# One transformer layer on one core: both input streams loaded ahead of every adaLN tile, and the tile groups put at fixed places among the products

## The chip, the core and the metric

The kernel runs on one core of one Trainium2 chip. The metric is the device time of one execution in microseconds (us), the median of several runs. The core has a matrix engine (PE, with PEld for its weight loads), a vector engine (DVE), a scalar engine (ACT), GpSimd (POOL), and a sync engine (SP) which here does nothing but issue loads. Each engine takes its own instructions strictly in the order in which the program lists them, and waits for the others by semaphores.

## The reference, cut to what matters

One layer over 256 latent tokens `x` and 256 context tokens `ctx` of width 2048, in float32:

```python
sh1, sc1, g1, sh2, sc2, g2 = adaln(c, w_ada, b_ada)        # split(silu(c) @ w_ada + b_ada, 6)
csh1, csc1, ... = adaln(c_ctx, w_ada, b_ada)
h  = rms_norm(x,   norm_mix_g) * (1 + sc1)  + sh1
hc = rms_norm(ctx, norm_mix_g) * (1 + csc1) + csh1
y, _ = neighbourhood_attention(h, hc, w_qkv, ...)          # q from h; k, v from h and hc; 16 heads
x = x + g1 * y
hf = rms_norm(x, norm_ffn_g) * (1 + sc2) + sh2
x = x + g2 * conv_ffn(hf, w_up, conv_w, conv_b, w_down)    # 5504 hidden columns
```

## The kernel before

Activations lie with features on the partitions: `xl` and `xc` hold the two streams as 16 feature tiles of 128 by 256 tokens. A product in full float32 precision is made of three fast ones: each weight tile `wr` is split on ACT into a rounded part `wh` (a CAST) and on DVE into a remainder `wl`; the activations are split in the same way into `hh` and `hl`; and PE adds up `wh*hh`, `wl*hh` and `wh*hl` (lines 369 to 371 in `nat`, 128x512 each). The tiles rotate: four buffers for `wr`, three for `wh`, two for `wl`.

The change concerns the first stage, the first 166 us or so. The 16 feature tiles are worked off in nine steps ("grains": two of one tile, then seven of two), because shift and scale of each come from `w_ada`, 1 MB per feature tile, and that is loaded on the way. For a grain:

- `ada_step` loads its four adaLN tiles `wx` (each a quarter of the input rows; four buffers) and multiplies them with silu(c) in four groups of small matmuls (line 404, called groups below). ACT copies the sums into `ev`, PE transposes them (line 414), and DVE reduces them to `shT` and `gsT` (lines 419 to 427).
- `modulate` scales the grain's part of `xl` and `xc` on DVE (line 438), and makes `hh` on ACT (443) and `hl` on DVE (444).
- `first_products` multiplies `hh` and `hl` with three weight tiles: the first 512 columns of k, kept in four PSUM banks `pj`, and the first 1024 of v, made in two rotating banks `mx` and added up on DVE into `vsum` (line 471; for the first grain ACT copies them, line 469). It has six pieces of two token tiles each: k for latent tokens, v0 latent, k context, v0 context, v1 latent, v1 context. A piece is 6 products for a grain of one tile, and 12 for a grain of two.

The groups of the next grain are written between the pieces of this one. `stats` computes 1/rms of a stream: squares on ACT (351), sums on DVE (356) and PE (226), the power on POOL (194), and a broadcast by PE (217). In the kernel before, `xl` is loaded first, then the first grain's `wx`, two weight tiles and only then `xc`; the first grain's pieces for latent tokens are multiplied while `xc` comes in and is normalized.

All loads of weights and streams go through one queue, SP's. The order on each engine is set by a scheduler at compile time, which goes by program order, by its own estimates of durations, and by the hints in the code (`issue_after`: not before that instruction of the same engine; `high_priority`).

Of the kernel before, what the change touches and what calls it, by code (L numbers as in the profile page):

```python
# [9 lines left out]
F32 = mybir.dt.float32  # L10
# [5 lines left out]
P = 128  # L16
# [36 lines left out]
def block_kernel(  # L53
# [23 lines left out]
    def ms():  # L77
        return ps.tile([P, CH], F32, tag="ms", name="ms", bufs=2)
# [65 lines left out]
        )  # L144
        return w

    last = []

    def wpair(src, k0, kn, c0, cn):

        w = wload(src, k0, kn, c0, cn)
        hi = wp.tile([P, KT, CH], F32R, tag="wh", name="wh", bufs=3)
        lo = wp.tile([P, KT, CH], F32R, tag="wl", name="wl", bufs=2)
        a = nc.scalar.copy(hi[:, :kn, :cn], w[:, :kn, :cn])  # L154
        b = nc.vector.tensor_tensor(  # L155
            out=lo[:, :kn, :cn], in0=w[:, :kn, :cn], in1=hi[:, :kn, :cn].bitcast(F32),
            op=ALU.subtract,
        )
        last[:] = [a.ins, b.ins]
        return hi, lo  # L160

# [42 lines left out]
    def rstd_rows(pool, sums, name, copy):  # L204

        v = pool.tile([P, 2], F32, tag=name + "v", name=name + "v")
        nc.vector.tensor_scalar(
            out=v, in0=sums, scalar1=1.0 / D, scalar2=EPS, op0=ALU.mult, op1=ALU.add
        )
        r = rsqrt_newton(pool, v, 2, name, 1)  # L210
        dg = pool.tile([P, 2, P], F32, tag=name + "d", name=name + "d")
        diag = nc.vector.tensor_tensor(
            out=dg, in0=ident.unsqueeze(1).to_broadcast([P, 2, P]),
            in1=r.unsqueeze(2).to_broadcast([P, 2, P]), op=ALU.mult,
        )
        bp = mx()[:, :T]
        nc.tensor.matmul(bp, ones, dg.rearrange("p b t -> p (b t)"), start=True, stop=True)
# [103 lines left out]
    def hl(kt, t):  # L321
        return hls[kt // (KD // 2)][:, kt % (KD // 2), t]
# [38 lines left out]
    def nat(psl, tt0, w, kt0, n, first, last):  # L361

        wh, wl = w
        for i, pt in enumerate(psl):
            ts = slice((tt0 + i) * P, (tt0 + i + 1) * P)
            for k in range(n):
                kt = kt0 + k
                a, z = first and k == 0, last and k == n - 1
                nc.tensor.matmul(pt, hh[:, kt, ts], wh[:, k, :], start=a, stop=False)  # L369
                nc.tensor.matmul(pt, hh[:, kt, ts], wl[:, k, :], start=False, stop=False)  # L370
                nc.tensor.matmul(pt, hl(kt, ts), wh[:, k, :], start=False, stop=z)  # L371
            side.tick(side.rate)
            ada.tick(ada.rate)

# [10 lines left out]
    kps = [pj() for _ in range(4)]  # L385
    loads = []

    def ada_step(b0, nb, work=()):

        ap_ = ms()  # L390
        n = 2 * nb * P
        for q in range(4):
            if q < len(work):
                work[q]()
            w = xp.tile([P, 4 * CH], F32, tag="wx", name="wx", bufs=4)[:, : 4 * n]
# [7 lines left out]
            for k in range(4):  # L403
                nc.tensor.matmul(  # L404
                    ap_[32 * k : 32 * k + 32, :n], s32[:, 4 * q + k, :], w[:, k * n : (k + 1) * n],
                    start=(q == 0), stop=(q == 3), tile_position=(0, 32 * k),
                )
        for piece in work[4:]:
            piece()
        ev = xp.tile([P, CH], F32, tag="ev", name="ev")  # L410
        nc.scalar.copy(ev[:, :n], ap_[:, :n])
        sp = ms()
        for b in range(2 * nb):
            nc.tensor.transpose(sp[:, b * P : (b + 1) * P], ev[:, b * P : (b + 1) * P], ident)
        blk = slice(b0, b0 + nb)
        spv = sp.rearrange("p (b g c) -> p b c g", g=4, c=32)
        for which, dst in ((0, shT), (1, gsT)):
            bcol = S_B + which * KD + b0
            nc.vector.tensor_reduce(
                out=dst[:, blk, :], in_=spv[:, which * nb : (which + 1) * nb, 0:2, :], axis=AX.X,  # L420
                op=ALU.add,
            )
# [10 lines left out]
    def modulate(b0, nb, streams=None):  # L433

        for st, x_ in streams or ((0, xl), (1, xc)):
            t = slice(st * T, (st + 1) * T)
            for kt in range(b0, b0 + nb):
                nc.vector.scalar_tensor_tensor(
                    out=x_[:, kt, :], in0=x_[:, kt, :], scalar=gsT[:, kt, st : st + 1], in1=rb[st],
                    op0=ALU.mult, op1=ALU.mult,  # L440
                )
                sh = shT[:, kt, st : st + 1]
                nc.scalar.activation(hh[:, kt, t], x_[:, kt, :], AF.Identity, bias=sh)  # L443
                nc.vector.scalar_tensor_tensor(
                    out=hl(kt, t), in0=x_[:, kt, :], scalar=sh, in1=hh[:, kt, t].bitcast(F32),
                    op0=ALU.add, op1=ALU.subtract,
                )


    vsums = [kv.tile([P, 4, CH], F32, tag=tag, name="vsum") for tag in ("qq", "kl")]  # L450
# [37 lines left out]
    modulate(*GRAINS[0], ((1, xc),))  # L488
    for j, grain in enumerate(GRAINS):
        work = first_products(*grain) if j else work[2:]  # L490
        if j + 1 < len(GRAINS):
            ada_step(*GRAINS[j + 1], work)
            modulate(*GRAINS[j + 1])
        else:
            for piece in work:
                piece()
    with tc.issue_after(loads[-1]):
        nc.sync.dma_start(rpd, rpv)
# [493 lines left out]
```

## Time and profile before

| | |
|---|---|
| median of 3 runs | 1412.73 us (1411.97 to 1412.95) |
| profiled execution: time, span | 1413.4 us, 1411.6 us |
| busy: PE, DVE, ACT, POOL | 98%, 73%, 49%, 4% of the span |
| moved from HBM | 312.75 MB, 224 GB/s over the span |
| mean granted PE clock | 0.997 of full speed |

The span runs from the first to the last instruction of the profiled execution. A row of the timeline reads: start in us, duration, engine, line, operation, written tile<-read tiles, shapes, and in brackets how long the engine had stood idle and what ended that. Durations of successive matmuls overlap, so the pace of PE is the distance of their starts. A group of four adaLN matmuls appears as x8, since a float32 matmul is run in two passes.

### The profile page before, as it was taken

What the parts mean: (1) busy time and instruction counts of PE and PEld (TensorE: products, weight loads), DVE (VectorE), ACT (ScalarE), POOL (GpSimd) and SP (SyncE); (2) the same over time, 40 slices, a digit from 0 to 9 for tenths busy, and PEclk for the clock granted to TensorE, in tenths of its full rate; (3) what the DMA queues carried; (4) which work ended last, traced back from release to release, by engine and by line L of the source; (5) the groups of instructions that cost most, each with busy time, mean ns of one, the idle gap of its engine ahead of it and who ended that gap; (6) DMA issues with size and microseconds to landing.
All of it is one profiled execution on the core that took longest, in us unless ns stands there. A gap on an engine that the chain in (4) does not pass through costs nothing.

```text
span 1411.6 us, 20931 instructions
## 1 busy us (share of the span) xinstructions
PE 1387.0 (98%) x7672; PEld 1167.5 (83%) x7672; DVE 1027.9 (73%) x1694; ACT 695.2 (49%) x1218; POOL 54.4 (4%) x57
## 2 busy tenths in 40 slices
PE   5999999999999999999999999999999999999998
PEld 2665778888888888888988888888888888888888
DVE  4555678879877978789797887878887675545454
ACT  4322254564444564554575555556555564333343
POOL 1000010120010020000000000000000000000000
PEclk9999999999999999999999999999999999999999
DMA  9998737768776868566767777777776666666554
GB/s 307 357 344 284 234 99 235 229 213 253 232 241 192 273 210 274 177 217 207 258 193 241 236 234 232 233 232 236 236 223 193 173 192 198 196 195 204 167 186 148
DMA packets 208919, 317.14 MB, mean 225 GB/s; under 512 B 23360, under 2 KB 87744, under 8 KB 208816
## 3 DMA queue, kind: packets, MB, share of 16 engines
q1 hardware_dynamic: 208688, 315.79, 72.0%
q8 instruction: 60, 0.98, 0.3%
q14 instruction: 43, 0.35, 0.1%
q10 hardware_dynamic: 128, 0.01, 0.0%
HBM read 312.75 MB, written 3.01 MB: 224 GB/s over the span
## 4 chain that ended last, share of the span: by engine, by line
PE 94%; DVE 3%; SPq 1%; DMA 1%; issue 0%; ACT 0%; DVEq 0%; ACTq 0%
PE pj L721 20%; PE pj L728 10%; PE mx L721 9%; PE pj L370 8%; PE pj L369 8%; PE pj L371 8%; PE ms L721 8%; PE mx L728 5%; PE ms L728 4%; PE mx L369 2%; PE ms L404 2%; PE mx L370 2%; PE mx L371 2%; SPq L398 1%; PE ms L624 1%; DVE wl L155 1%
## 5 line engine op out<-in xcount | busy, mean ns | idle before, releaser
L155 DVE TENSOR_TENSOR wl<-wr,wh 128x1024 fp32r<-128x1024 f32 (+2 forms) x425 | 478.1, 1125 | 270.7 <-PE pj L728 98.1
L154 ACT CAST wh<-wr 128x1024 fp32r<-128x1024 f32 (+2 forms) x425 | 412.9, 972 | 531.4 <-PE pj L721 162.0
L370 PE MATMUL pj<-wl,hh 128*128 128x512 f32 x512 | 203.1, 397 | 0.0
L371 PE MATMUL pj<-wh,hl 128*128 128x512 f32 x512 | 200.2, 393 | 0.0
L369 PE MATMUL pj<-wh,hh 128*128 128x512 f32 x512 | 193.7, 397 | 2.4 <-ACT hh L443 2.4
L271 DVE SCALAR_TENSOR_TENSOR acc<-wa,sT,acc 128x512 f32<-128x512 f32 x240 | 183.4, 766 | 3.3 <-DMA wa<-in_w_ada 0.8
L721 PE MATMUL pj<-hf,wh 128*128 128x512 f32 x624 | 158.3, 392 | 0.0
L721 PEld LDWEIGHTS pj<-hf,wh 128*128 128x128 f32 x624 | 112.1, 189 | 19.9
L369 PEld LDWEIGHTS pj<-wh,hh 128*128 128x128 f32 x512 | 96.0, 189 | 26.6 <-issue 3.4
L370 PEld LDWEIGHTS pj<-wl,hh 128*128 128x128 f32 x512 | 96.8, 189 | 21.5 <-DVE wl L155 0.9
L371 PEld LDWEIGHTS pj<-wh,hl 128*128 128x128 f32 x512 | 96.5, 188 | 18.9
L721 PE MATMUL mx<-hf,wh 128*128 128x512 f32 x352 | 97.5, 394 | 0.0
L721 PE MATMUL ms<-hf,wh 128*128 128x512 f32 x336 | 90.8, 390 | 0.0
L728 PEld LDWEIGHTS pj<-hf,wl 128*128 128x128 f32 x624 | 84.8, 190 | 6.0
L728 PE MATMUL pj<-hf,wl 128*128 128x256 f32 x624 | 88.0, 283 | 0.0
L721 PEld LDWEIGHTS ms<-hf,wh 128*128 128x128 f32 x336 | 63.1, 188 | 14.2
L471 DVE TENSOR_TENSOR vsum<-vsum,mx 128x512 f32<-128x512 f32 x64 | 43.1, 682 | 34.3 <-PE mx L371 34.1
L721 PEld LDWEIGHTS mx<-hf,wh 128*128 128x128 f32 x352 | 60.6, 190 | 7.8
L728 PEld LDWEIGHTS mx<-hf,wl 128*128 128x128 f32 x352 | 53.7, 189 | 6.8
L728 PE MATMUL mx<-hf,wl 128*128 128x256 f32 x352 | 55.9, 282 | 0.0
L728 PE MATMUL ms<-hf,wl 128*128 128x256 f32 x336 | 54.7, 283 | 0.0
L369 PE MATMUL mx<-wh,hh 128*128 128x512 f32 x128 | 53.1, 415 | 0.3 <-DVE vsum L471 0.2
(264 smaller groups left out, 2070.7 us busy)
## 6 DMA issues: line engine op xcount, KB each, us to landing
wr<-in_w_up SPq DMA_DIRECT2D x160, 512.0 KB, 4.4
wa<-in_w_ada SPq DMA_DIRECT2D x128, 512.0 KB, 4.8
wr<-in_w_qkv SPq DMA_DIRECT2D x93, 512.0 KB, 4.4
wr<-in_w_down SPq DMA_DIRECT2D x63, 512.0 KB, 4.7
wx<-in_w_ada SPq DMA_DIRECT2D x56, 512.0 KB, 8.6
wr<-in_w_o SPq DMA_DIRECT2D x24, 512.0 KB, 5.0
wr<-in_w_down SPq DMA_DIRECT2D x45, 256.0 KB, 3.0
wr<-in_w_up SPq DMA_DIRECT2D x16, 384.0 KB, 3.3
```

What stands on the lines that cost most here:

```text
L154: a = nc.scalar.copy(hi[:, :kn, :cn], w[:, :kn, :cn])
L155: b = nc.vector.tensor_tensor(out=lo[:, :kn, :cn], in0=w[:, :kn, :cn], in1=hi[:, :kn, :cn].bitcast(F32), op=ALU.subtract,)
L271: nc.vector.scalar_tensor_tensor(out=acc, in0=w[:, k, :], scalar=s, in1=acc, op0=ALU.mult, op1=ALU.add)
L369: nc.tensor.matmul(pt, hh[:, kt, ts], wh[:, k, :], start=a, stop=False)
L370: nc.tensor.matmul(pt, hh[:, kt, ts], wl[:, k, :], start=False, stop=False)
L371: nc.tensor.matmul(pt, hl(kt, ts), wh[:, k, :], start=False, stop=z)
L398: load = nc.sync.dma_start(w.rearrange("p (k s f) -> p k s f", k=4, s=2)[:, :, which, :], w_ada[q * CH : (q + 1) * CH, c0 : c0 + n // 2].r ...
L404: nc.tensor.matmul(ap_[32 * k : 32 * k + 32, :n], s32[:, 4 * q + k, :], w[:, k * n : (k + 1) * n], start=(q == 0), stop=(q == 3), tile_pos ...
L471: nc.vector.tensor_add(acc[:, h0 + i, :], acc[:, h0 + i, :], pr_[i])
L624: nc.tensor.transpose(tp[:, kt * P : (kt + 1) * P], pr[:, kt * P : (kt + 1) * P], ident)
L721: nc.tensor.matmul(pts[b][:, : m.shape[-1]], wh[:, k, bs], m, start=(kt == 0 and t.start == 0), stop=False,)
L728: nc.tensor.matmul(pts[b][:, : m.shape[-1]], wl[:, k, bs], m, start=False, stop=(kt == kn - 1))
```

## The change

Five edits. (1) `xc` is loaded directly behind `xl`, ahead of all adaLN tiles, and both streams are normalized first. (2) For the two grains of one tile, two quarters of the adaLN tile share one buffer, so the second grain's loads don't wait for a buffer. (3) `ada_load` issues a grain's loads apart from `ada_step`, ahead of its products. (4) In the first grain the CAST and the remainder of the first two weight tiles (`wpair`) are held behind the copy to `ev` and the last scaling (`hold`), and `modulate` has priority. (5) For the next three steps a table, `BEHIND`, says after how many of the six pieces each of the four groups is multiplied. The arithmetic is the same, and so are the numbers of products, groups and bytes.

```diff
+BEHIND = {0: (3, 3, 4, 4), 1: (2, 3, 5, 6), 2: (2, 2, 4, 5)}
...
     def wpair(src, k0, kn, c0, cn):
...
+        with ExitStack() as order:
+            for ins in hold:
+                order.enter_context(tc.issue_after(ins))
+            a = nc.scalar.copy(hi[:, :kn, :cn], w[:, :kn, :cn])
+            b = nc.vector.tensor_tensor(
+                out=lo[:, :kn, :cn], in0=w[:, :kn, :cn], in1=hi[:, :kn, :cn].bitcast(F32),
+                op=ALU.subtract,
+            )
...
-    def ada_step(b0, nb, work=()):
+    def ada_load(b0, nb):
+        n, ws = 2 * nb * P, []
         for q in range(4):
+            if nb == 2 or q % 2 == 0:
+                slot = xp.tile([P, 4 * CH], F32, tag="wx", name="wx", bufs=4)
+            w = slot[:, 4 * n * (q % 2) : 4 * n * (q % 2 + 1)] if nb == 1 else slot
...
+    def ada_step(ws, b0, nb, work=(), behind=None):
+        for q, w in enumerate(ws):
+            with ExitStack() as order:
+                for piece in work[done : behind[q] if behind else q + 1]:
+                    piece()
+                    done += 1
+                if behind or not work and q > 1:
+                    order.enter_context(tc.issue_after(last_mm[0]))
                 for k in range(4):
+                    mm = nc.tensor.matmul(
...
+        with ExitStack() as order:
+            if behind:
+                order.enter_context(tc.issue_after(mm.ins))
+            for piece in work[done:]:
+                piece()
+        with ExitStack() as order:
+            if behind or not work:
+                order.enter_context(tc.high_priority())
+            return ada_end(ap_, b0, nb)
...
     stream(xl, xT)
-    rb = [stats(xl, "x")[0]]
-    ada_step(*GRAINS[0])
+    stream(xc, ctxT)
+    tiles = ada_load(*GRAINS[0])
+    rb = [stats(xl, "x")[0], stats(xc, "c")[0]]
+    copied = ada_step(tiles, *GRAINS[0])
+    with tc.high_priority():
+        scaled = modulate(*GRAINS[0])
+    hold[:] = [copied, scaled]
     ahead()
-    stream(xc, ctxT)
-    modulate(*GRAINS[0], ((0, xl),))
-    work = first_products(*GRAINS[0])
-    work[0]()
-    work[1]()
-    rb.append(stats(xc, "c")[0])
-    modulate(*GRAINS[0], ((1, xc),))
+    hold.clear()
     for j, grain in enumerate(GRAINS):
-        work = first_products(*grain) if j else work[2:]
         if j + 1 < len(GRAINS):
-            ada_step(*GRAINS[j + 1], work)
-            modulate(*GRAINS[j + 1])
+            tiles = ada_load(*GRAINS[j + 1])
+            ada_step(tiles, *GRAINS[j + 1], first_products(*grain), BEHIND.get(j))
+            with ExitStack() as order:
+                if j in BEHIND:
+                    order.enter_context(tc.high_priority())
+                modulate(*GRAINS[j + 1])
```

Three places in the engines' orders. A row is line, operation, written tile<-read tile, elements, and how often in a row; a number behind a name tells one tile from the next of its kind. Lines move by 2 to 39 (404 becomes 429, 411 448, 414 451, 443 481, 471 510).

The first is the head of the loading queue, SP, before:

```order
L344 DMA xl<-in_xT 128x4x256 x4
L398 DMA wx<-in_w_ada 128x4x128 x8
L141 DMA wr<-in_w_qkv 128x512 x2
L344 DMA xc<-in_ctxT 128x4x256 x4
L141 DMA wr<-in_w_qkv 128x512 x2
L398 DMA wx<-in_w_ada 128x4x128 x8
```

and now:

```order
L350 DMA xl<-in_xT 128x4x256 x4
L350 DMA xc<-in_ctxT 128x4x256 x4
L405 DMA wx<-in_w_ada 128x4x128 x8
L143 DMA wr<-in_w_qkv 128x512 x2
L405 DMA wx<-in_w_ada 128x4x128 x8
L143 DMA wr<-in_w_qkv 128x512 x2
```

The context stream moved ahead of ten loads, and the third and fourth weight tiles moved behind the second grain's eight adaLN loads.

The second is the head of ACT behind the squares of `xl`, before:

```order
L154 CAST wh<-wr 128x512 x2
L411 COPY ev<-ms 128x256
L351 ACTIVATE sq<-xc 128x512 x3
L443 ACTIVATE hh<-xl,shT 128x256
L351 ACTIVATE sq<-xc 128x512 x5
L154 CAST wh<-wr 128x512
L469 COPY vsum<-mx 128x512 x2
```

and now:

```order
L357 ACTIVATE sq<-xc 128x512 x8
L448 COPY ev<-ms 128x256
L159 CAST wh<-wr 128x512 x3
L481 ACTIVATE hh<-xl,shT 128x256
L481 ACTIVATE hh<-xc,shT 128x256
L508 COPY vsum<-mx 128x512 x2
```

The CASTs of three weight tiles, not of two, now stand between the copy to `ev` and the first grain's `hh`, and the third is of a tile that SP loads behind the second grain's `wx`. Before, the third stood behind `hh` of the latent tokens.

The third is the end of the second grain, where the third grain's last group, its transposes and its first products follow. On PE before (`mx_430`, `mx_431` and `mx_460` are v products of the second grain):

```order
L404 MATMUL ms_404<-wx_470,s32_118 32x512 x4
L369 MATMUL mx_431<-wh_407,hh_109 128x512
L370 MATMUL mx_431<-wl_408,hh_109 128x512
L371 MATMUL mx_431<-wh_407,hl0_110 128x512
L369 MATMUL mx_460<-wh_407,hh_109 128x512
L370 MATMUL mx_460<-wl_408,hh_109 128x512
L371 MATMUL mx_460<-wh_407,hl0_110 128x512
L414 MATMUL ms_505<-ident_71,ev_503 128x128 x4
L369 MATMUL mx_461<-wh_407,hh_109 128x512
L370 MATMUL mx_461<-wl_408,hh_109 128x512
L371 MATMUL mx_461<-wh_407,hl0_110 128x512
L369 MATMUL mx_483<-wh_426,hh_109 128x512
```

and now:

```order
L377 MATMUL mx<-wh,hl_110 128x512
L429 MATMUL ms<-wx,s_118 32x512 x4
L451 MATMUL ms<-ident,ev 128x128 x4
L375 MATMUL pj<-wh,hh 128x512
L376 MATMUL pj<-wl,hh 128x512
```

Before, six products stand between the last group and the transposes, and twelve more and a group behind the transposes, ahead of the third grain's first `pj`; now there are none. On DVE, in the middle of the same grain, now:

```order
L510 TENSOR_TENSOR vsum_130<-vsum_130,mx_455 128x512
L160 TENSOR_TENSOR wl_468<-wr_465,wh_467 128x1024
L510 TENSOR_TENSOR vsum_130<-vsum_130,mx_456 128x512
L510 TENSOR_TENSOR vsum_131<-vsum_131,mx_471 128x512
L510 TENSOR_TENSOR vsum_131<-vsum_131,mx_472 128x512
```

The remainder of a double weight tile of the third grain, `wl_468`, stands between two of the sums that free the banks `mx` for `mx_471` and `mx_472`.

More of the change, by code (lines that the diff above doesn't have):

```diff
@@ L145, in wload @@
         return w
-    last = []
+    last, last_mm, hold = [], [], []
     def wpair(src, k0, kn, c0, cn):
@@ L216, in rstd_rows @@
         bp = mx()[:, :T]
-        nc.tensor.matmul(bp, ones, dg.rearrange("p b t -> p (b t)"), start=True, stop=True)
+        mm = nc.tensor.matmul(bp, ones, dg.rearrange("p b t -> p (b t)"), start=True, stop=True)
+        last_mm[:] = [mm.ins]
         rb = pool.tile([P, T], F32, tag=name + "b", name=name + "b")
@@ L402, in ada_step, with ada_end @@
             loads.append(load.ins)
[L403 to L409, printed above, removed]
+            ws.append(w)
+        return ws
+    def ada_step(ws, b0, nb, work=(), behind=None):
+        ap_ = ms()
+        n = 2 * nb * P
+        done = 0
+        for q, w in enumerate(ws):
[5 more added lines that the diff above has]
+                    order.enter_context(tc.issue_after(last_mm[0]))
+                for k in range(4):
+                    mm = nc.tensor.matmul(
+                        ap_[32 * k : 32 * k + 32, :n], s32[:, 4 * q + k, :],
+                        w[:, k * n : (k + 1) * n], start=(q == 0), stop=(q == 3),
+                        tile_position=(0, 32 * k),
+                    )
+        with ExitStack() as order:
[7 more added lines that the diff above has]
+            return ada_end(ap_, b0, nb)
+    def ada_end(ap_, b0, nb):
+        n = 2 * nb * P
         ev = xp.tile([P, CH], F32, tag="ev", name="ev")
-        nc.scalar.copy(ev[:, :n], ap_[:, :n])
+        copied = nc.scalar.copy(ev[:, :n], ap_[:, :n])
         sp = ms()
@@ L431, in ada_step, with modulate @@
         )
-    def modulate(b0, nb, streams=None):
-        for st, x_ in streams or ((0, xl), (1, xc)):
+        return copied.ins
+    def modulate(b0, nb):
+        for st, x_ in ((0, xl), (1, xc)):
             t = slice(st * T, (st + 1) * T)
             for kt in range(b0, b0 + nb):
-                nc.vector.scalar_tensor_tensor(
+                scaled = nc.vector.scalar_tensor_tensor(
                     out=x_[:, kt, :], in0=x_[:, kt, :], scalar=gsT[:, kt, st : st + 1], in1=rb[st],
```

16 lines of the change are left out of this document (4 added, 12 removed).

## The prediction

> **What bounds the kernel now.** The page comes first: its busy shares, the slices, the chain of waits.
>
> ```profile
> PE 1387.0 (98%) x7672; PEld 1167.5 (83%) x7672; DVE 1027.9 (73%) x1694; ACT 695.2 (49%) x1218; POOL 54.4 (4%) x57
> PE   5999999999999999999999999999999999999998
> ...
> DMA  9998737768776868566767777777776666666554
> ...
> PE 94%; DVE 3%; SPq 1%; DMA 1%; issue 0%; ACT 0%; DVEq 0%; ACTq 0%
> ```
>
> PE is busy in every slice but the first, and is 94% of the chain that ends last. A busy PE need not be a dense one, so next the waits of PE from 42.4 us to the end (engine, tile, line, what was waited for: total us, times, longest):
>
> ```profile
> PE ms L728 <- DVE wl L155: 2.4, 4, 1.0
> PE pj L721 <- ACT wh L154: 0.8, 1, 0.8
> PE mx L369 <- DVE vsum L471: 0.2, 1, 0.2
> ```
>
> That is 3.4 us in 1369: whatever is lost ahead of 42 us is paid in full at the end, and nothing can be gained behind it. What is to be had lies in the head, shown here by stretches (busy us and instructions of PE, PEld, DVE, ACT, POOL; then granted PE clock, DMA share, GB/s):
>
> ```profile
> 12.40:23.20 10.80, 7.64 (x44) 3.51 (x44) 5.27 (x17) 3.71 (x8) 0.71 (x1) 1.00 1.12 330
> 23.20:28.80 5.60, 5.57 (x16) 3.96 (x20) 4.06 (x7) 3.74 (x7) 0.00 (x0) 1.00 1.13 321
> 28.80:32.20 3.40, 2.28 (x28) 1.36 (x28) 0.92 (x5) 0.60 (x2) 0.70 (x1) 1.00 1.18 295
> 32.20:39.05 6.85, 6.35 (x27) 3.47 (x20) 3.72 (x13) 1.69 (x4) 0.00 (x0) 0.50 1.08 351
> 39.05:42.40 3.35, 3.35 (x19) 1.80 (x19) 1.29 (x3) 2.11 (x4) 0.00 (x0) 1.00 1.10 345
> ```
>
> Loads are saturated throughout (295 to 351 GB/s, share above 1), so there the queue decides when a thing can begin.
>
> **Part 1: when the first product can start.** The head's timeline gives the pace of the queue, from ACT and PE instructions that waited for a landing:
>
> ```profile
> 10.57 1.15 ACT L351 ACTIVATE sq<-xl 128x512 f32<-128x512 f32 x2 [0.37 <-DMA xl<-in_xT]
> ...
> 17.79 0.23 PEld L404 LDWEIGHTS ms<-wx,s 128*32 128x32 f32 x8 [1.49 <-DMA wx<-in_w_ada]
> ...
> 18.39 1.31 ACT L154 CAST wh<-wr 128x512 fp32r<-128x512 f32 x2 [6.67 <-DMA wr<-in_w_qkv]
> ...
> 20.64 1.15 ACT L351 ACTIVATE sq<-xc 128x512 f32<-128x512 f32 x2 [0.66 <-DMA xc<-in_ctxT]
> ...
> 22.15 0.63 ACT L351 ACTIVATE sq<-xc 128x512 f32<-128x512 f32 x1 [0.36 <-DMA xc<-in_ctxT]
> ...
> 22.68 0.49 ACT L443 ACTIVATE hh<-xl,shT 128x256 fp32r<-128x256 f32 x1
> ...
> 23.23 0.79 PE L369 MATMUL pj<-wh,hh 128*128 128x512 f32 x1 [2.45 <-ACT hh L443]
> ...
> 26.21 0.60 ACT L154 CAST wh<-wr 128x512 fp32r<-128x512 f32 x1
> ```
>
> Tiles land one behind the other in the order of issue. A quarter of a stream takes 1.5 us (20.64 to 22.15), the eight loads of a one-tile grain 7.2 (10.57 to 17.79), a weight tile of 128x512 0.6 to 0.7 (17.79 to 18.39). In the new order: `xl` to 10.5 as now; `xc` 4 x 1.5, to 16.5; the first `wx` to 23.7; two weight tiles to 25.1; the second grain's `wx` to 32.3; the third weight tile to 33.0. The third CAST stands ahead of `hh` on ACT, so it holds `hh` although `ev`, the scaling and both first weights are long done: 33.0 + 0.60 (CAST) + 0.5 (`hh`) = 34.1, first product 34.15, instead of 23.2. Both streams' statistics, moved ahead, cost nothing: `xc` is there 16 us before that, and the statistics of `xl` took 10 us from its landing at 10.5 to its first scaling; without this cover they would cost as much. POOL's power for `xc` only comes earlier.
>
> What PE must do from there to reach the state that it has at 40.34 now is priced by these rows of PE:
>
> ```profile
> 24.25 0.63 PE L369 MATMUL pj<-wh,hh 128*128 128x512 f32 x1
> 24.67 0.63 PE L370 MATMUL pj<-wl,hh 128*128 128x512 f32 x1
> ...
> 27.66 1.05 PE L371 MATMUL mx<-wh,hl 128*128 128x512 f32 x2
> 28.65 0.69 PE L404 MATMUL ms<-wx,s 128*32 128x256 f32 x8
> ...
> 30.25 0.64 PE L404 MATMUL ms<-wx,s 128*32 128x256 f32 x8
> ...
> 35.99 0.80 PE L369 MATMUL pj<-wh,hh 128*128 128x512 f32 x1
> ...
> 39.11 0.39 PE L370 MATMUL mx<-wl,hh 128*128 128x512 f32 x1
> ...
> 40.34 1.07 PE L404 MATMUL ms<-wx,s 128*32 128x512 f32 x8
> ...
> 42.60 0.40 PE L370 MATMUL mx<-wl,hh 128*128 128x512 f32 x1
> 42.83 0.39 PE L371 MATMUL mx<-wh,hl 128*128 128x512 f32 x1
> ```
>
> At 40.34 it has done 24 products, the second grain's four groups and their transposes. At the later pace (42.60 to 42.83: 0.23 each) that is 24 x 0.23 = 5.5, four groups at 0.65 = 2.6, transposes 0.3: 8.4 us, to 42.5. **+2.2.**
>
> **Part 2: the slow clock at the start.** The twelve products from 23.23 to 28.65 run at 0.43 us each (24.25 to 24.67), and again the seven from 35.99 to 39.11; the granted clock of the stretch 32.2 to 39.05 is 0.50. The new start comes out of a pause on PE, too. Bounds: seven products lose 7 x 0.2 = 1.4, twelve 2.4. I take 12, the row of the first start, which like the new one follows no dense stretch: **+2.4.**
>
> **Part 3: holes in the second grain.** These rows price the links from groups to products, and the vector work between them:
>
> ```profile
> 20.82 0.17 DVE L419 TENSOR_REDUCE shT<-ms 128x2 f32<-128x8 f32 x1
> ...
> 21.49 0.48 DVE L438 SCALAR_TENSOR_TENSOR xl<-xl,gsT,xb 128x256 f32<-128x256 f32 x1
> ```
> ```profile
> 51.25 0.59 ACT L411 COPY ev<-ms 128x512 f32<-128x512 f32 x1 [0.19 <-PE ms L404]
> ...
> 52.60 0.60 PE L414 MATMUL ms<-ident,ev 128*128 128x128 f32 x4
> ...
> 53.41 0.17 DVE L419 TENSOR_REDUCE shT<-ms 128x4 f32<-128x16 f32 x1
> ```
> ```profile
> L471 DVE TENSOR_TENSOR vsum<-vsum,mx 128x512 f32<-128x512 f32 x43 | 29.0, 683 | 30.6 <-PE mx L371 30.6
> L155 DVE TENSOR_TENSOR wl<-wr,wh 128x1024 fp32r<-128x1024 f32 x15 | 18.3, 1222 | 14.2 <-PE mx L370 10.2 <-issue 2.5 <-ACT ev L411 1.0
> ```
>
> First, the second grain's `hh` after its transposes: reduce to scaling 0.7, scaling 0.5, `hh` 0.5, some 0.1 between, 1.8 in all, of which six products hide 1.4; ACT may put a copy to `vsum` ahead. **+0.6** (0.3 to 1.0).
>
> Second, DVE's order of sum, remainder, sum. PE writes `mx_471` only when the sum of `mx_455` is done, 0.2 us after it wants to; and `mx_472` only when `mx_455`'s sum, the remainder and `mx_456`'s sum are: 0.17 + 0.68 + 1.22 + 0.68 = 2.75 behind the last product of `mx_455`, while PE has six products (1.4) to go on with. **+1.3** together (zero if the remainder comes early).
>
> Third, the last group of the third grain, with nothing behind it on PE but its own transposes: 0.2 + 0.6 (`ev`) + 0.6 (transposes) + 0.2 (to the reduce) + 0.7 + 0.5 + 0.5 + 0.1 = 3.4, less the 0.6 of the transposes: **+2.8** (2.4 to 3.1). Today 18 products and a group cover this chain; its cover is gone here alone, since after the first grain twelve products stand behind the last group, and after the third one piece of twelve.
>
> **Part 4: the clock again.** After that hole products may start at half clock: 0 if they don't, 2.4 if twelve of them do as at 23.23, 1.4 for seven as at 35.99. I take **+1.7**, nearer to the second, since the pause is short. A page of the Trainium skill, "TensorE: Matmul & The Clock Gate" (section "Part 1: The HAM clock gate"), has the clock fall only after about 3.4 us of idleness, and rise after as long a busy time; by that the hole of 2.8 would not suffice and the sum be 8.3. Here the clock stood at 0.50 from 32.2 although groups ran at 28.65 and 30.25, so I go by the row.
>
> **Part 5: groups put together.** Of the groups of 128x512, PE's order has 26 separate rows before and 22 now. Two in one cost 1.92 against 2 x 1.07:
>
> ```profile
> 86.75 1.92 PE L404 MATMUL ms<-wx,s 128*32 128x512 f32 x16
> ```
>
> With the edge to the products, 0.25 each: **-1.0** (0 to -1.4).
>
> At nothing I cost the rest: the shared `wx` buffers (the second grain's loads no longer wait, but they land in the same queue), the later issue of the loads from the third grain on, which wait for a buffer until a group placed later is multiplied (a grain of two takes 8 x 1.5 us of `wx` and about 4 of weights in the queue, against 72 x 0.23 + 4 x 1.07 + 0.6 = 21.5 of PE; if this cover of 5 us is used up, PE waits), and the other grains' order.
>
> **The sum:** 2.2 + 2.4 + 0.6 + 1.3 + 2.8 + 1.7 - 1.0 = +10.0 on the profiled 1413.4, which stands 0.7 above the median of the runs; from that, 1412.7 + 10.0 = 1422.7, I say 1423. The terms' bounds give +4.9 to +12.4, 1417.6 to 1425.1.
>
> **The rivals.**
> (A) The third weight tile lands ahead of the second grain's `wx`. Then `hh` follows `ev`; in today's first grain the first product comes 5.4 us behind the last landing of `wx` (17.79 to 23.23), so at 23.7 + 5.4 = 29.1, 5.0 sooner than above: 1418. Against it: every row above lands in order. The Trainium skill ("DMA: Bandwidth & Descriptors", section "Queues, rings and completion order") says that completion within one issuing engine's queue isn't first in, first out; that rule is this rival. The weight tile that ACT waits for at 18.39, behind eight loads issued before it, speaks for the order.
> (B) The loss is given back later: a stage behind 166 us would have PE waiting for others anyway, and a late PE would find them ready. It decides from 7.2 us of such waits on, which brings the sum within 2.8; all of 10.0 gives 1412.7, no slower. Against it, the waits from 42.4 on are 3.4 in all.
> (C) Loads from the fourth grain on come late, since SP waits for buffers freed by groups placed later: half of four loads of 512 KB at 1.5 us, twice, is 6 more: 1429.
> (D) The change does what it says, with (A) and a full clock and no holes: 29.1 + 8.4 = 37.5, 2.8 ahead, and 1.0 from part 5: 1409. It needs four things at once.
>
> **How the numbers follow.** A measurement of this kernel can tell about 0.2%, 2.8 us, from no change. The likeliest case has 0.66, with 1417.6 to 1426 as its own range (a landing later than by these paces included); (A) 0.12, (C) 0.12, (B) 0.06, (D) 0.04. Slower: 0.66 + 0.12 + 0.12 = 0.90; the same: (B), 0.06; faster: (D), 0.04. The range from 1417 to 1429 holds the likeliest case, (A), and part of (C).
>
> **What would show it.** On ACT the third CAST should begin near 33.0, ended by a weight's landing, and `hh` right behind it; the first product near 34.1, at starts 0.43 apart until 38 to 41; a wait of PE for `vsum` of about 1 us near 58; and idle PE for nearly 3 us around the third grain's transposes near 65, with half clock behind it. Waits of PE behind 80 us should be as now. A first product before 31, a wait for `wx` behind 70, or waits behind 166 that shrink by more than 3 would prove it wrong.

## The result, and the profile after

The changed kernel takes 1425.1 us (median of 5 runs, 1424.7 to 1426.0) against 1412.7: ratio 1.0089, 95% interval 1.0077 to 1.0101. It is slower by 12.4 us, in the upper half of what was forecast (1423, range 1417 to 1429). Its profiled execution took 1424.7, with a span of 1422.7. First the page of the changed kernel:

```profile
PE 1386.9 (97%) x7672; PEld 1168.9 (82%) x7672; DVE 1030.1 (72%) x1694; ACT 695.2 (49%) x1218; POOL 58.4 (4%) x57
PE   3899999999999999999999999999999999999998
```

PE's busy time is what it was, 1386.9 for 1387.0; its span is 11.1 longer. So on balance the loss is idle time, and what slow or badly packed stretches add to the busy time is made up elsewhere. In slices of 35.6 us PE falls from 5 and 9 tenths to 3 and 8 in the first two, up to 71 us, and nowhere else. The waits of PE from 42.4 us to the end say how much is plain waiting (engine, tile, line, what was waited for: total us, times, longest):

```profile
PE ms L770 <- DVE wl L160: 2.4, 4, 1.0
PE pj L375 <- ACT hh L481: 2.2, 2, 1.8
PE ms L429 <- DMA wx<-in_w_ada: 1.8, 1, 1.8
PE pj L763 <- DVE om L601: 0.8, 1, 0.8
PE mx L375 <- DVE vsum L510: 0.8, 1, 0.8
PE ms L451 <- ACT ev L448: 0.7, 1, 0.7
```

Four of the six rows are new or (`vsum`, 0.2 before) longer, 5.5 us in all. The first and the fourth lie behind 166 us, where PE waited 2.4 and 0.8 before, too, so nothing is given back there. The timeline shows where the new ones stand; first ACT and PE at the start:

```profile
28.75 1.14 ACT L159 CAST wh<-wr 128x512 fp32r<-128x512 f32 x2
32.73 0.62 ACT L159 CAST wh<-wr 128x512 fp32r<-128x512 f32 x1 [2.84 <-DMA wr<-in_w_qkv]
33.25 0.50 ACT L481 ACTIVATE hh<-xl,shT 128x256 fp32r<-128x256 f32 x1
```
```profile
33.80 1.22 PE L375 MATMUL pj<-wh,hh 128*128 128x512 f32 x2 [4.15 <-ACT hh L481]
...
39.73 1.07 PE L429 MATMUL ms<-wx,s 128*32 128x256 f32 x16
...
42.34 1.07 PE L429 MATMUL ms<-wx,s 128*32 128x256 f32 x16
43.34 0.50 PE L375 MATMUL mx<-wh,hh 128*128 128x512 f32 x1
...
47.02 0.50 PE L375 MATMUL pj<-wh,hh 128*128 128x512 f32 x1 [0.38 <-ACT hh L481]
57.05 0.50 PE L375 MATMUL mx<-wh,hh 128*128 128x512 f32 x1 [0.77 <-DVE vsum L510]
60.53 1.06 PE L429 MATMUL ms<-wx,s 128*32 128x512 f32 x8
62.30 0.66 PE L451 MATMUL ms<-ident,ev 128*128 128x128 f32 x4 [0.71 <-ACT ev L448]
64.76 0.80 PE L375 MATMUL pj<-wh,hh 128*128 128x512 f32 x1 [1.80 <-ACT hh L481]
65.35 0.63 PE L376 MATMUL pj<-wl,hh 128*128 128x512 f32 x1
...
67.91 0.43 PE L376 MATMUL mx<-wl,hh 128*128 128x512 f32 x1
92.44 1.07 PE L429 MATMUL ms<-wx,s 128*32 128x512 f32 x8 [1.81 <-DMA wx<-in_w_ada]
```

The third CAST waits for its weight's landing and holds `hh`; the first product comes at 33.80, the 25th at 43.34. The first eight run slowly, about 0.43 apart, though the clock column of the profile has 1.00 there:

```profile
34.00:37.30 3.30, 3.30 (x8) 2.62 (x9) 0.68 (x2) 0.16 (x1) 0.00 (x0) 1.00 1.09 348
```

The clock's record begins at 37.3 us in this trace, and at 28.8 in that of the kernel before; ahead of that the column shows nothing, and the pace of the products has to be read. Then come the wait for `hh` at 47.0, the one for `vsum` at 57.1, the hole around the third grain's transposes (idle 0.71 + 1.80), and eight products at 0.43 each from 64.76 to 67.91. The last row, a wait for `wx` at 92.44, the prediction had said would not be there. Its cause stands on SP's queue and in the stretches from 62 on (busy us and instructions of PE, PEld, DVE, ACT, POOL; then PE clock, DMA share, GB/s):

```profile
62.67 0.46 SPq L143 DMA_DIRECT2D wr<-in_w_qkv  x1
73.98 2.02 SPq L405 DMA_DIRECT2D wx<-in_w_ada  x4
```
```profile
62.00:66.00 4.00, 1.90 (x7) 1.47 (x8) 3.30 (x12) 1.95 (x5) 0.00 (x0) 0.82 1.09 351
66.00:70.00 4.00, 4.00 (x14) 3.16 (x14) 0.93 (x3) 0.00 (x0) 0.00 (x0) 0.75 0.85 284
70.00:80.00 10.00, 10.00 (x57) 6.32 (x55) 3.75 (x5) 1.40 (x2) 0.00 (x0) 1.00 0.51 162
```

SP issues nothing for 11 us, because the next `wx` wants a buffer whose group the table places late; from 70 to 80 the queue moves 162 GB/s, less than half of the 351 from 62 to 66.

The products of 128x512 can be counted in every trace, and their starts compared. Behind the first 24 the changed kernel is 2.0 us late (43.3 against 41.3), behind 72 it is 6.7, behind 144 it is 12.4, and from 432 products on (171.4 against 182.8) it keeps 11.3 to 11.4 to the last product. This count places a loss without the scatter of the last stage (1 to 2 us), so it stands beside the times below. It is taken from one execution of each kernel, and has in it how long the products of that execution ran slowly at the start.

### The profile page after: what moved, and what is told of

It reads as the page before. It is cut to its first block, busy times and chain, and to the rows that moved or that the text cites. A ratio compares the mean times of both kernels' runs of the same rounds, so it can differ in the third digit from the quotient of the medians.

```text
span 1422.7 us, 20925 instructions
## 1 busy us (share of the span) xinstructions
PE 1386.9 (97%) x7672; PEld 1168.9 (82%) x7672; DVE 1030.1 (72%) x1694; ACT 695.2 (49%) x1218; POOL 58.4 (4%) x57
## 4 chain that ended last, share of the span: by engine, by line
PE 94%; DVE 2%; SPq 2%; DMA 1%; issue 0%; ACT 0%; DVEq 0%
PE pj L763 20%; PE pj L770 10%; PE mx L763 9%; PE pj L375 8%; PE pj L376 8%; PE pj L377 8%; PE ms L763 8%; PE mx L770 5%; PE ms L770 4%; PE mx L375 2%; PE ms L429 2%; PE mx L376 2%; PE mx L377 2%; SPq L405 1%; PE ms L666 1%; DVE wl L160 1%
```

## The experiments

The theory: the holes and waits that the fixed places bring cost more (7.8 us) than the late start (3.2). The rival: the late start carries the loss, and the holes follow from it. Each kernel was timed 4 to 11 times; the ratios are against the kernel before on the same chip. The last column is the start of the product behind the 432nd.

| kernel | us | ratio, 95% interval | behind 432 |
|---|---|---|---|
| before | 1412.7 to 1413.6 | | 171.4 |
| changed | 1425.1 | 1.0089 (1.0077 to 1.0101) | 182.8 |
| no_table | 1415.8 | 1.0016 (1.0007 to 1.0025) | 172.5 |
| table_alone | 1423.5 | 1.0071 (1.0059 to 1.0084) | 181.4 |
| own_wx | 1421.7 | 1.0059 (1.0047 to 1.0072) | 179.2 |
| cast_behind_hh | 1424.2 | 1.0073 (1.0059 to 1.0086) | 181.2 |
| first_row_only | 1416.2 | 1.0017 (1.0009 to 1.0026) | 175.1 |
| second_row_only | 1417.4 | 1.0029 (1.0018 to 1.0039) | 175.2 |
| third_row_only | 1419.7 | 1.0051 (1.0038 to 1.0063) | 176.1 |
| first_row_hh_early | 1414.8 | 1.0011 (1.0002 to 1.0019) | 172.2 |
| groups_in_hole | 1421.4 | 1.0062 (1.0050 to 1.0075) | 178.5 |
| first_two_rows | 1425.4 | 1.0089 (1.0076 to 1.0103) | 182.7 |
| no_table_hh_early | 1414.8 | 1.0015 (1.0006 to 1.0024) | 172.5 |
| whole_groups | 1419.5 | 1.0052 (1.0039 to 1.0066) | 176.6 |

### The change in two halves

**no_table:** the new head without the fixed places.

```diff
-BEHIND = {0: (3, 3, 4, 4), 1: (2, 3, 5, 6), 2: (2, 2, 4, 5)}
+BEHIND = {}
```

> The changed kernel with an empty table: nothing is placed by hand, the scheduler sets groups and pieces of the first three grains as it did before; loads, statistics, shared buffers and the hold on the first weights stay. Theory (the fixed places cost most): the trace of the changed kernel shows behind the 24th product the wait for hh 0.5, the waits for vsum 1.2, the hole at the third grain's transposes 2.7, the half clock behind it 1.6 and the wait for wx at 92.44 of 1.8, in all 7.8; without the table they are gone. The first product still starts at 33.8, since the third CAST still stands ahead of hh. In PE's order the second grain's sixteen groups now stand ahead of the first product, so their 2.0 us fall into that wait: 1425.1 - 7.8 - 2.0 = 1415.3, range 1413.5 to 1418. Rival (the late start carries the loss, and the holes follow from loads bunched behind it): first product and holes both stay, 1422 or more.

**table_alone:** the kernel before with the fixed places.

```diff
+BEHIND = {0: (1, 1, 2, 2), 1: (2, 3, 5, 6), 2: (2, 2, 4, 5)}
...
-            ada_step(*GRAINS[j + 1], work)
-            modulate(*GRAINS[j + 1])
+            ada_step(*GRAINS[j + 1], work, BEHIND.get(j))
+            with ExitStack() as order:
+                if j in BEHIND:
+                    order.enter_context(tc.high_priority())
+                modulate(*GRAINS[j + 1])
```

> The kernel before with the table alone: the first three steps' groups at the same fixed places behind pieces (counted without the two pieces that it issues ahead of the loop), priority for what follows the last group; loads and statistics stay where they were, no shared buffers. Theory (the fixed places cost most): first product at 23.2 as before, then the same holes: 1412.7 + 7.8 = 1420.5, range 1418 to 1424; the hole at the third grain's transposes of 2 to 3 us and half clock behind it must be there. Rival (the late start carries the loss): no hole, since all loads are there earlier; 1411 to 1415.

By the ratios the halves came out at +2.3 us (0.16%) and +10.0 (0.71%), together 12.3 of the 12.6 (0.89%) of the whole. The table brings its losses without the new head: PE's timeline of the run with the table alone has the same hole, and the same slow pace behind it.

```profile
39.68 1.07 PE L412 MATMUL ms<-wx,s 128*32 128x256 f32 x16
...
42.34 0.50 PE L371 MATMUL mx<-wh,hh 128*128 128x512 f32 x1
...
61.30 0.66 PE L433 MATMUL ms<-ident,ev 128*128 128x128 f32 x4 [0.71 <-ACT ev L430]
63.76 0.79 PE L371 MATMUL pj<-wh,hh 128*128 128x512 f32 x1 [1.80 <-ACT hh L462]
64.35 0.63 PE L372 MATMUL pj<-wl,hh 128*128 128x512 f32 x1
```

Its time, 1423.5, lies 3.0 above its expectation, since the theory had no price for the table in the head. The first two rows show one: before, the second grain's groups ran from 28.65 to 35, while `xc` was still being normalized; here they stand between products, two together at 39.68 and two at 41.34, and the state that the kernel before had at 40.34 comes at 42.34, with the transposes still to come. That is 2.3 late, though the first product starts at 23.59.

And the new head without the table starts as late, at 34.38, yet loses 1.1 by the product count. PE's timeline of that run shows why:

```profile
29.10 3.00 PE L429 MATMUL ms<-wx,s 128*32 128x256 f32 x24
32.72 0.64 PE L429 MATMUL ms<-wx,s 128*32 128x256 f32 x8 [0.62 <-DMA wx<-in_w_ada]
34.38 0.73 PE L375 MATMUL pj<-wh,hh 128*128 128x512 f32 x2 [1.02 <-ACT hh L481]
```

The second grain's four groups run inside the wait for `hh`, where the first row of the table doesn't let them. In this execution the half clock fell into the same wait, too (0.50 from 28.8 to 32.2), and the products started at full pace; where it falls differs from trace to trace. The rival falls: it had the holes stay, and 1422 or more.

### The late start by itself

**own_wx:** each quarter of a one-tile grain has a buffer of its own again.

```diff
-            if nb == 2 or q % 2 == 0:
-                slot = xp.tile([P, 4 * CH], F32, tag="wx", name="wx", bufs=4)
-            w = slot[:, 4 * n * (q % 2) : 4 * n * (q % 2 + 1)] if nb == 1 else slot
+            w = xp.tile([P, 4 * CH], F32, tag="wx", name="wx", bufs=4)[:, : 4 * n]
```

> The changed kernel, but each wx tile of a one-tile grain has a buffer of its own, as before, in place of two in one. Table, loads ahead and all else stay. SP's order then has all four first weight tiles ahead of the second grain's wx, since those must wait for the first grain's groups. Theory: the third CAST no longer waits for a landing at 33.0, hh follows the scaling that ended at 30.84, the first product stands at 31.3 in place of 33.8; all that follows keeps its distance: 1425.1 - 2.5 = 1422.6, range 1420.5 to 1424. Rival (the shared buffers only move a wait: the second grain's wx land later and its groups take the time): 1424.5 to 1426.5.

**cast_behind_hh:** `modulate` also returns `hh`'s instruction, and `hold` keeps later CASTs and remainders behind it.

```diff
+        scaled, rounded = modulate(*GRAINS[0])
     hold[:] = [copied, scaled]
     ahead()
-    hold.clear()
+    hold[:] = [rounded]
```

> The changed kernel, with the third and later CASTs of the head held behind the first grain's hh on ACT; loads, shared buffers and table stay. Theory: hh follows the scaling that ended at 30.84, first product at 31.3 in place of 33.8, though the third weight still lands at 33.0: it is wanted only by later products; 1425.1 - 2.5 = 1422.6, range 1420.5 to 1424. Rival (the start doesn't matter, a later landing sets the pace, so that PE waits there instead): first product at 31.3 too, but 1424.5 to 1426.

Both put the first product 3 us earlier, at 30.93 and 30.69. ACT in the two runs:

```profile
28.48 1.66 ACT L159 CAST wh<-wr 128x512 fp32r<-128x512 f32 x3
30.37 0.51 ACT L479 ACTIVATE hh<-xl,shT 128x256 fp32r<-128x256 f32 x1 [0.24 <-DVE xl L474]
```
```profile
30.13 0.51 ACT L481 ACTIVATE hh<-xl,shT 128x256 fp32r<-128x256 f32 x1 [0.99 <-DVE xl L476]
...
32.95 0.62 ACT L159 CAST wh<-wr 128x512 fp32r<-128x512 f32 x1 [1.91 <-DMA wr<-in_w_qkv]
```

So the shared buffers, costed at nothing by themselves, are what let the second grain's `wx` be issued ahead of the third weight, and so the cause of the late start: without them SP has all four first weights in front, and the three CASTs run in one. That is worth 3.6 behind 432 products (3.4 in time), 2.9 of it at the 25th product (40.45 for 43.34). Not all of the rest need come from the buffers: the adaLN groups of 128x512 were busy 30.3 us here and 31.3 in the changed kernel, which a later section explains. With the hold on ACT the same 3 us were won at the start, but 1.6 is left behind 432 products, and 0.8 in time, less than was expected: the first 24 products took 0.5 longer at the slow clock, and the wait for `wx` near 90 grew from 1.81 to 2.38; half a microsecond more goes between the 144th and the 432nd product and is unplaced. The rest of the miss in time is within the runs' scatter (1422.1 to 1425.2).

### The table's rows, one by one

```diff
-BEHIND = {0: (3, 3, 4, 4), 1: (2, 3, 5, 6), 2: (2, 2, 4, 5)}
+BEHIND = {0: (3, 3, 4, 4)}
+BEHIND = {1: (2, 3, 5, 6)}
+BEHIND = {2: (2, 2, 4, 5)}
```

The three lines with a plus are one kernel each: **first_row_only**, **second_row_only**, **third_row_only**.

> The changed kernel with the table's first row alone (places in the first grain's pieces); the second and third grains' pieces are placed by the scheduler. Theory (each row costs what stands at its places): beside the kernel without a table, 1415.8, the second grain's sixteen groups go back behind the first products (2.0, no longer inside the wait for hh) and the wait for hh of 0.4 to 0.5 behind its transposes comes back: 1418.2, range 1416.5 to 1420; no hole near 64, no wait for wx behind 80. Rival (the rows act only together, the first one sets up the hole of the next): 1420 or more.

> The changed kernel with the table's second row alone. Theory: the hole at the third grain's transposes (2.7, of it 0.7 for ev and 1.8 for hh), the half clock behind it (1.6) and the waits for vsum (1.2) are all its own: 1415.8 + 5.5 = 1421.3, range 1418.5 to 1422.5; the wait for wx near 92 is absent. Rival (the hole comes from the late landing of the third grain's wx, which the first row pushes): no hole, 1414.5 to 1417.

> The changed kernel with the table's third row alone. In the changed kernel SP issued nothing from 62.67 to 73.98, since the next wx wait for a buffer of a group placed late, and the queue stood empty from 70.48 to 77.60 less one landing of 1.5: 5.6 us. PE paid 1.8 of it at 92.44. Theory: the queue loses the same here, but PE has not been held by the second row's holes, so more of the loss reaches it: 1.8 to 1.8 + 5.6, 1415.8 + 5 = 1421, range 1418 to 1423.5, as one wait for wx between 75 and 100. Rival (the terms add, 1.8 is the row's price): 1417.0 to 1418.

The first row alone costs 2.6 behind 432 products against no table, near the expected 2.5, but that is partly luck, and its time hardly moved (1416.2 for 1415.8, under the range; the ratios are 1.0017 and 1.0016). The expected wait for `hh` did not come back: from its first product to the 432nd, no wait of PE shows in that run. Instead 14 products from 34.83 on ran slowly, about 0.43 apart, and none without the table, while fewer groups were parted (29.4 us of busy time for 30.9; a later section explains it). And its profiled execution is the slowest of 11 (1418.2), the other one among the faster (1414.6). So what the first row costs under the new head is not shown. The second row's expectation failed: 2.7 in place of 5.5. PE's timeline of that run at the transposes:

```profile
59.74 0.66 PE L451 MATMUL ms<-ident,ev 128*128 128x128 f32 x4 [0.71 <-ACT ev L448]
60.33 1.92 PE L429 MATMUL ms<-wx,s 128*32 128x512 f32 x16
62.20 0.50 PE L375 MATMUL pj<-wh,hh 128*128 128x512 f32 x1
```

Without the third row the scheduler sets two of the fourth grain's groups into the hole; there is no wait for `hh`, and no slow clock behind it. So the hole belongs to the second and third rows together: one takes the products away, the other the groups. The third row alone lost 3.6, neither theory's way: PE paid 1.73 for `wx` (at 86.79), as the rival had it, and 1.64 for a remainder `wl` at 58.27 with 0.8 for `vsum`, which neither had. Its time lies in the theory's range, but not for the theory's reason.

**groups_in_hole:** two numbers of the whole table, so that two groups may stand there again.

```diff
-BEHIND = {0: (3, 3, 4, 4), 1: (2, 3, 5, 6), 2: (2, 2, 4, 5)}
+BEHIND = {0: (3, 3, 4, 4), 1: (2, 3, 5, 6), 2: (0, 0, 4, 5)}
```

> The changed kernel with two numbers of the table changed: the fourth grain's first two groups stand ahead of the third grain's pieces (0, 0 in place of 2, 2), so right behind the third grain's transposes, in the hole that the changed kernel shows from 62.96 to 64.76. Theory (the hole is there because the second row leaves no product and the third row no group for it; the clock falls because of it): 1.92 of groups take the place of the wait of 1.8 for hh, the clock stays at 1.00 behind it (1.6 kept), the wait for wx of 1.8 stays or shrinks, since the buffers come free earlier: 1425.1 - 3.4 = 1421.7, down to 1419.9 with that wait gone; range 1419 to 1422.8. Rival (groups don't hold the clock, as at 32.2 in the kernel before, where it stood at 0.50 although groups ran): wait gone, half clock still behind it, 1423.3.

```profile
62.79 0.66 PE L451 MATMUL ms<-ident,ev 128*128 128x128 f32 x4 [0.71 <-ACT ev L448]
63.38 1.92 PE L429 MATMUL ms<-wx,s 128*32 128x512 f32 x16
65.25 0.50 PE L375 MATMUL pj<-wh,hh 128*128 128x512 f32 x1
```

Wait and half clock are both gone, with 4.3 us behind 432 products and 3.7 in time. SP goes on to the next `wx` at 64.51 instead of 73.98, and the wait for `wx` shrinks from 1.8 to 0.7.

### A loss that no wait shows

**first_two_rows:** the whole table but its third row, `BEHIND = {0: (3, 3, 4, 4), 1: (2, 3, 5, 6)}`.

> The changed kernel without the table's third row. Theory (the hole and its half clock belong to the second and third rows together, the rest adds): at the 432nd product the runs with one row stood 2.6 (first) and 2.7 (second) behind the run without a table, that one 1.1 behind the kernel before; 1.1 + 2.6 + 2.7 = 6.4 on 1413.4: 1419.8, range 1418 to 1421.5; no hole over 1 us near 64, no half clock there, no wait for wx behind 80. Rival (the first row pushes the second's hole back in): hole and half clock, 1422 to 1424.

It took 1425.4, a miss by 5.6, although there is no hole at 64, no half clock, and one wait for `wx` of 1.2 at 66.78. From 67 us to 162 no wait of PE shows. So the question was what a busy PE did. The groups, gathered by line from 60 to 183 us, of this run:

```profile
L429 PE MATMUL ms<-wx,s 128*32 128x512 f32 x200 | 30.6, 602 | 1.2 <-DMA wx<-in_w_ada 1.2
```

The four matmuls of a group stand side by side in the array (128*32, each at its own `tile_position`), and a whole group, eight records (two for each matmul), takes 1.06. Where the scheduler puts products in between, a part takes as long: in the changed kernel's own timeline two of eight records last 1.04, four 1.05, ten as long as sixteen:

```profile
120.34 1.04 PE L429 MATMUL ms<-wx,s 128*32 128x512 f32 x2
...
122.90 1.92 PE L429 MATMUL ms<-wx,s 128*32 128x512 f32 x16
...
125.19 1.05 PE L429 MATMUL ms<-wx,s 128*32 128x512 f32 x4
...
127.53 1.91 PE L429 MATMUL ms<-wx,s 128*32 128x512 f32 x10
```

Counting each piece as so many eights, rounded up, the 224 records of this size make 28 if none is parted; before it is 29, in the changed kernel 31, here 33.

**whole_groups:** the same kernel, with the second to fourth matmul of a group tied to the first.

```diff
                 for k in range(4):
+                    with ExitStack() as whole:
+                        if k:
+                            whole.enter_context(tc.issue_after(first.ins))
+                            whole.enter_context(tc.high_priority())
                         mm = nc.tensor.matmul(
...
+                        first = first if k else mm
```

> The run with the table's first two rows, in which the scheduler no longer parts the four products of a group: the second to fourth follow the first with priority. In its trace a part of a group lasts as long as a whole one (at 106.59 two of eight records take 1.04 us, at 104.94 six of eight 1.06, where a whole one takes 1.07), and 224 records stand in pieces of 33 times eight or fewer, where 28 would do. Theory (the miss of that run, 1425.4 for 1419.8, is parted groups): 5 x 0.86 (two groups in one 1.92, less 1.06 for one) = 4.3, and four edges fewer, 26 to 22 pieces, 0.8 to 1.0: 1425.4 - 5.2 = 1420.2, range 1418.5 to 1422. Rival (the parts run beside the products between them, and cost nothing; the miss is the late start and the wait for wx at 66.78): 1424.5 to 1426.

```profile
L433 PE MATMUL ms<-wx,s 128*32 128x512 f32 x200 | 25.6, 602 | 1.5 <-DMA wx<-in_w_ada 1.5
```

5.0 us less for the same 200 records, and 6.0 in time (6.1 behind 432 products, of which 0.9 is an earlier start). So parted groups cost 5.0 in that run. They were not all new in it: the 224 records were busy for 33.8 us there, but for 30.9 without a table, 29.4 with the first row alone and 31.1 with the second. The sum of single rows that the expectation rests on would have 29.6, so some 4 of the miss are put down to groups parted only when both rows stand together; the wait for `wx` of 1.2 is new, too. Why the scheduler parts more of them when the first two rows are placed by hand was not tried.

### A version ahead of both

**first_row_hh_early** (first row alone, with the hold of cast_behind_hh) and **no_table_hh_early** (that hold, no table):

> A version meant to beat both: the table's first row alone, and the third and later CASTs of the head behind the first grain's hh on ACT. Theory: first product at 30.7 as in the run with that hold, three us ahead of the run with the first row alone: 1418.2 - 3.0 = 1415.2, range 1413 to 1417; that is no better than the kernel before (1413.1), since the new head reaches the 24th product at 40.7 against 41.3. Rival (the freed start is kept in full and the first row costs nothing without the others): 1410 to 1412.5, ahead of both.

> No table, and the third and later CASTs of the head behind the first grain's hh on ACT: the best that the runs so far point to. Theory: the first product may start 3 us earlier than without that hold (34.4), but PE's order has the second grain's sixteen groups ahead of it, the last of which waits for a landing at 32.7 in the run without a table; so about 1 us is won: 1414.7, range 1413 to 1416, no better than the kernel before at 1413.4. Rival (all of the 3 us reach the end): 1411.5 to 1412.7, ahead of both kernels.

Both times came as the theory had them, and neither kernel is ahead of the one before: the intervals begin above 1. The second was to gain about 1 us, and gains nothing behind 432 products over the run without that hold (172.5 both), since PE's order has the second grain's groups first and these wait for their own landing. Whole groups in the kernel before, which has 29 where 28 would do, were not tried; an estimate from the rows above (28.8 us of busy time for the 224 records in whole_groups, 30.3 before) is one to one and a half microseconds.

## Why the prediction was right, point by point

The side and the size were right, and six of its seven terms are found in the trace at the places where it put them; that the sum comes so near is partly luck, as shown below. In the order of its steps:

| term | predicted | in the trace of the changed kernel |
|---|---|---|
| late first product, slow clock behind it | +2.2, +2.4 | +3.2 together |
| `hh` behind the second grain's transposes | +0.6 | +0.4 |
| sum, remainder, sum | +1.3 | +1.0 |
| hole at the third grain's transposes | +2.8 | +2.5 |
| half clock behind it | +1.7 | +1.6 |
| groups put together | -1.0 | about +0.1 |
| wait for `wx` at 92.44 | 0 | +1.8 |
| sum | +10.0 | +10.6 |

The terms from the late product to the half clock were put too high, by 2.3 together, and the last two too low, by 2.9; the sum is near because these errors nearly cancel. The span is 11.1 longer, so half a microsecond is unplaced. The medians lie 12.4 apart, mostly since the profiled execution stood 0.7 above the median before and stands 0.4 below it now.

**The late start.** The chain was right: queue order, third CAST, `hh`; the CAST began at 32.73 for 33.0 predicted, the product at 33.80 for 34.15. Mis-sized was the way from there to the state that the kernel before had at 40.34: the 25th product starts at 43.34, which with the transposes still to come is 3.2 late, not 4.6. Eight products ran slow, not twelve, and a pair of small groups together took 1.0, not 1.3 (39.73 to 40.73). Rival (A), the weight ahead of the `wx`, did not come: all tiles landed in the order of issue. What the prediction did not see is that the late first product need not cost this much: no_table pays 1.1 for the same start, since groups and slow clock fall into the wait, and under the old head the table is 2.3 late at the same place with an early first product. How much of the 3.2 is the first row's stays open, since by time its run and no_table don't differ. Slow products at the start differ from trace to trace, too: eight here, 14 in first_row_only, none in no_table.

**The holes.** All three are where they were put, and within 0.3. The experiments add whose the largest is: it needs two rows of the table, and is gone when either is.

**The clock.** The row of the kernel before was the right guide. By the Trainium skill ("TensorE: Matmul & The Clock Gate", section "Part 1: The HAM clock gate") the clock gate looks at a free-running window of 3413 ns, and lowers the clock after an idle one; the prediction took from it that a hole of 2.8 would not suffice, and put 8.3 beside 10.0. The window shows in this trace, too: the clock fell for 3.41 us. But it fell without an idle window, and here the measurement decides. Windows of that length in the changed kernel:

```profile
61.15:64.56 3.41, 1.10 (x11) 0.42 (x4) 2.71 (x10) 1.46 (x3) 0.00 (x0) 1.00 1.08 355
64.56:67.98 3.42, 3.22 (x8) 2.55 (x9) 2.37 (x7) 1.34 (x4) 0.00 (x0) 0.50 1.09 354
67.98:71.39 3.41, 3.41 (x16) 2.79 (x15) 0.00 (x0) 0.00 (x0) 0.00 (x0) 1.00 0.36 128
```

PE was busy for 1.10 us of the first window, 0.66 of it with transposes, and the clock stood at 0.50 for the whole next one. The same page (section "Part 4: PE-mode transpose") says that a transpose doesn't count as busy in the same way; by that 0.44 would be left. Busy time alone does not decide, as two such windows of own_wx show, with the same 1.61 us of busy PE:

```profile
59.49:62.90 3.41, 1.61 (x9) 1.20 (x10) 2.74 (x11) 1.60 (x4) 0.00 (x0) 1.00 1.08 362
86.79:90.20 3.41, 1.61 (x20) 0.32 (x12) 3.37 (x9) 1.70 (x4) 0.00 (x0) 1.00 1.06 337
```

Behind the first, with 0.56 of transposes and the rest products, the clock fell to 0.50; behind the second, with groups alone, it stayed at 1.00. That agrees with the page on transposes, but the other matmuls of the two windows differ as well, so the runs don't show which of them counts. Where groups filled the hole (groups_in_hole), it stayed at 1.00.

**Groups put together** was the step that failed by sign. The count of separate rows, 26 to 22, was right and brings four edges fewer, but it overlooked that a row can hold part of a group, which costs as much as a whole one. The busy time of the 224 records rose:

```profile
L404 PE MATMUL ms<-wx,s 128*32 128x512 f32 x224 | 30.3, 603 | 0.0
```
```profile
L429 PE MATMUL ms<-wx,s 128*32 128x512 f32 x224 | 31.3, 602 | 1.8 <-DMA wx<-in_w_ada 1.8
```

One microsecond more, less about 0.9 for the edges: nothing saved.

**Later loads, costed at nothing.** Here the step "this cover of 5 us" failed, as far as a test of the prediction's own said: a wait for `wx` behind 70 would prove it wrong. The cover compared the queue's work for a grain with PE's, and left out that SP stands still until a buffer is free: 11 us without an issue, of which PE paid 1.8. It is rival (C), at under a third of the size that it was given. The likeliest case held, with this part of (C) on top and the -1.0 missing.

**Rivals (B) and (D).** Nothing was given back behind 166 us: the waits there stayed at 2.4 and 0.8, and the distance of 11.4 behind 432 products is 11.3 at the last one. (D) needed four things, none of which came.

## What to carry to other kernels

An order fixed by hand has a cost at each place where it forbids a filler: before a row of such a table is kept, ask for each wait on the busiest engine which independent work the scheduler had put there, and whether two rows together take all of it away. Loads wait with the work that frees their buffers, so moving a consumer back moves a load back, and the queue's idle time shows it long before any wait does. And when an engine is busy in the whole stretch and the time still grows, compare the busy time of the same instructions: work that runs side by side in the array must stay side by side.

## What the runs showed of the hardware

A part of a group of four 128*32 matmuls of 512 columns takes as long as the whole group: two of eight records 1.04 us, all eight 1.06, sixteen 1.92; the 200 records from 60 us on took 30.6 us when often parted and 25.6 when never. And the granted clock fell by half for one window of 3.41 us after a window in which PE was busy for 1.10 us, 0.66 of it with transposes. In own_wx it fell after 1.61 us of products and transposes, and not after 1.61 of groups alone. SP's loads, 684 in each trace here, all landed in the order of issue, and a load whose buffer was not free held all loads behind it: SP issued nothing for 11 us.
